# Another order for the first four k-tiles of a two-layer decoder trunk

## The chip, the cores and the metric

The kernel runs on one core of one Trainium2 chip. The metric is the device time of one execution in microseconds; lower is better. A core has TensorE (matrix products into PSUM), VectorE, ScalarE and GpSimd (elementwise work) and SyncE, whose queue issues the DMA transfers here. Each engine runs its instructions in the order in which they stand in its queue and waits at semaphores for the others. In the profile PE is TensorE, PEld its weight loads, DVE VectorE, ACT ScalarE, POOL GpSimd and SPq the DMA issues of SyncE. L508 is line 508 of the kernel.

## What is computed

Two layers on x of 512 tokens by 2048 features, in float32. The opening, which is what the change touches, is the first layer's input projection with an adaptive shift and scale:

```python
c_act = jax.nn.silu(c)
mod = c_act @ w_mod[l] + b_mod[l]
shift, scale, gate = jnp.split(mod, 3, axis=-1)
h = x * (1.0 + scale[:, None]) + shift[:, None]
# layer 0, inside diff_attention:
proj = h @ w_in                              # 2048 x 8192
q, k, v, g = jnp.split(proj, 4, axis=-1)     # 8 heads; then attention, out projection
x = layer_norm(DN_ALPHA * x + gate[:, None] * y, ln_g[l], ln_b[l])
```

Layer 0 goes on with differential attention, an output projection and a layer norm; then come shared keys, values and forget gates and a second layer of attention.

## The kernel before

*Products.* The 2048 input features are 16 k-tiles of 128. To keep float32 accuracy each operand is split into an upper part, rounded to the fast matmul type, and a lower part, the rest; a product is three matmuls, upper-upper, upper-lower and lower-upper (L173, L174, L175, `products`). The upper part of a weight is a ScalarE cast (`whi`, L93), the lower a VectorE subtraction (`wlo`, L94), both in `WeightStream.step`, for two k-tiles at a time. Weights stream from memory through four staging buffers `wst` (loads at L46); `whi` and `wlo` have three buffers each.

*Shift and scale.* c_act @ w_mod is a sum over 16 k-tiles of rows of w_mod, each weighted by one column of c_act. The 16 k-tiles of output columns are cut into nine sets: sets 0 and 1 make one k-tile's shift and scale each, sets 2 to 8 two. A set's rows come in two or four tiles `sms` (L454; five buffers). VectorE multiplies each of the 16 row blocks by its column of c_act and adds (L479, L481, `sacc`; below, a step). TensorE then sums `sacc` over the partitions with a column of ones (L511, "last sums") and VectorE adds the bias (`mcol`, L517). In set 1 eight of the 16 row blocks are not done on VectorE but on TensorE, as matmuls of 128 by 128 with one column of c_act (L508, `on_pe`); such a matmul appears as two loads and two matmuls in the trace.

*h.* A k-tile of x (loaded as `xt`, L430) is turned by four transposes into PSUM (L522, `turn_x`); ScalarE applies shift and scale twice, to the upper part `hh` (L526) and to `htmp` (L527), and VectorE subtracts for the lower part `hl` (L531, `lower_h`).

*The opening's order.* Two head groups (u = 0 and 1) are computed there, each with seven accumulators of 512 columns in seven of the eight PSUM banks: three for q and k (banks `sc`, `sc`, `o`), four for v and gate (`acc`). One k-tile of one group is 7 accumulators by 3 matmuls, 21. Because the banks hold one group at a time, work runs in five phases, (group, first k-tile, end): (0, 0, 4), (1, 0, 8), (0, 4, 12), (1, 8, 16), (0, 12, 16). At a phase's end the accumulators are spilled: copied to SBUF by ScalarE the first time (L559), added by VectorE later (L561). The eighth bank, `tr`, serves transposes and sums.

VectorE's instructions run in the order in which the program writes them. That order is the string START: a digit is so many steps of the shift and scale sums, `c` the sums of the next set on TensorE, `m` its columns, `t` the turn of the next k-tile of x (with its set's sums, if they are still to be done), `l` a lower part of h, `s` the split of the next weights, `g` the products of the next k-tile of the running phase. All other engines are put in order by a planner from the program's order and its own estimates of time.

The mark T4, which the prediction uses, is the start of the first matmul of phase (1, 0, 8), that is, the end of the first four k-tiles of group 0.

## Time and profile before

| | us |
|---|---|
| median of 3 runs (2008.10 to 2009.01) | 2008.82 |
| the profiled execution, its own time | 2007.0 |
| its span, first to last instruction | 2005.2 |
| TensorE busy in it | 1964.4 (98%) |
| VectorE busy in it | 1336.4 (67%) |
| GpSimd busy in it | 2.2 |

How to read what the prediction shows. A row of a timeline is: start, length, engine, line, operation, what is written and read with shapes, how many instructions, and in brackets the idle time before it and what ended it. Lengths of TensorE are modelled and overlap, so costs are read from starts. A row of a table by stretches is: stretch, its length, then busy time and instruction count of PE, PEld, DVE, ACT and POOL, then the granted TensorE clock (1.00 is full), the mean busy share of the DMA engines and GB/s. A row without brackets whose engine field is followed directly by a tile's name ("PE tr L511 x8") is a piece of the chain of work that ended last: start, length, engine, tile, line, count.

### The profile page before, as it was taken

The numbers are of one execution on the slowest core, as the hardware profiler recorded it, in microseconds if no ns is written. First come the engines' busy times: TensorE is split into PE (matmuls) and PEld (weight loads), VectorE is DVE, ScalarE is ACT, GpSimd is POOL, SyncE is SP. The second block draws the span as 40 slices with busy tenths as digits, with TensorE's granted clock in tenths as the row PEclk, the third lists the DMA queues.
The fourth block names the chain that finished last, engine by engine and source line by source line (L and its number), as shares of the span: only waits on it lengthen the run. The fifth ranks groups of instructions, "written<-read, shape, count | busy, mean of one in ns | idle before, by whom it ended". The sixth has DMA issues, their size and how long they took to land.

```text
span 2005.2 us, 25007 instructions
## 1 busy us (share of the span) xinstructions
PE 1964.4 (98%) x9115; PEld 1626.3 (81%) x9115; DVE 1336.4 (67%) x2435; ACT 725.0 (36%) x1234; POOL 2.2 (0%) x10
## 2 busy tenths in 40 slices
PE   5999999999999999999999999999999999999997
PEld 4888878888888888888878888888888888888885
DVE  7887865677777778853576666635455555576778
ACT  2422445333333334431263222224343334353132
POOL 0000000000000000000000000000000000000000
PEclk8999999999999999999999999999999999999999
DMA  9994742375757666453336687634323232333755
GB/s 343 347 315 145 243 151 85 106 230 185 225 178 231 189 223 213 158 166 100 121 137 223 234 276 260 225 95 129 103 90 105 95 102 93 96 120 97 257 190 175
DMA packets 263095, 353.79 MB, mean 176 GB/s; under 512 B 18022, under 2 KB 162556, under 8 KB 262204
## 3 DMA queue, kind: packets, MB, share of 16 engines
q1 hardware_dynamic: 260592, 347.99, 53.2%
q10 hardware_dynamic: 2380, 4.21, 0.6%
q8 instruction: 71, 1.16, 0.2%
q14 instruction: 52, 0.43, 0.1%
...
## 4 chain that ended last, share of the span: by engine, by line
PE 90%; DVE 4%; DMA 3%; SPq 1%; issue 1%; ACT 0%; DVEq 0%; ACTq 0%
PE acc L173 26%; PE acc L174 26%; PE acc L175 26%; DMA ms<-in_w_mod_dram 2%; PE sc L173 2%; PE sc L174 2%; PE sc L175 2%; PE o L175 1%; PE o L174 1%; PE o L173 1%; PE tr L1200 1%; DVE macc L391 1%; DVE wlo L94 1%; DMA sms<-in_w_mod_dram 1%; PE tr L727 0%
## 5 line engine op out<-in xcount | busy, mean ns | idle before, releaser
L94 DVE TENSOR_TENSOR wlo<-wst,whi 128x1024 fp32r<-128x1024 f32 (+2 forms) x339 | 404.7, 1196 | 278.3 <-ACT whi L93 266.8
L93 ACT CAST whi<-wst 128x1024 fp32r<-128x1024 f32 (+2 forms) x339 | 349.6, 1032 | 641.0 <-PE acc L175 323.0
L173 PE MATMUL acc<-whi,hh 128*128 128x512 f32 x1252 | 491.7, 396 | 0.9 <-ACT hh L967 0.8
L174 PE MATMUL acc<-wlo,hh 128*128 128x512 f32 x1252 | 489.1, 391 | 0.0
L175 PE MATMUL acc<-whi,hl 128*128 128x512 f32 x1252 | 488.2, 390 | 0.0
L173 PE MATMUL acc<-hh,whi 128*128 128x512 f32 x1184 | 470.4, 397 | 1.1 <-DVE sg L680 0.6
L175 PE MATMUL acc<-hh,wlo 128*128 128x512 f32 x1184 | 462.3, 390 | 0.0
L174 PE MATMUL acc<-hl,whi 128*128 128x512 f32 x1184 | 462.2, 390 | 0.0
L391 DVE SCALAR_TENSOR_TENSOR macc<-ms,cact,macc 128x512 f32<-128x512 f32 x300 | 225.0, 750 | 78.7 <-DMA ms<-in_w_mod_dram 53.8
L175 PEld LDWEIGHTS acc<-whi,hl 128*128 128x128 f32 x1252 | 235.3, 188 | 50.7 <-DVE hl L968 0.3
L173 PEld LDWEIGHTS acc<-whi,hh 128*128 128x128 f32 x1252 | 235.7, 188 | 48.5 <-ACT hh L967 1.2
L174 PEld LDWEIGHTS acc<-wlo,hh 128*128 128x128 f32 x1252 | 235.6, 188 | 46.4 <-DVE wlo L94 0.4
L175 PEld LDWEIGHTS acc<-hh,wlo 128*128 128x128 f32 x1184 | 222.3, 188 | 48.6
L173 PEld LDWEIGHTS acc<-hh,whi 128*128 128x128 f32 x1184 | 222.6, 188 | 43.8 <-PE acc L175 1.0
L174 PEld LDWEIGHTS acc<-hl,whi 128*128 128x128 f32 x1184 | 222.8, 188 | 39.3
L481 DVE SCALAR_TENSOR_TENSOR sacc<-sms,cact,sacc 128x512 f32<-128x512 f32 (+1 forms) x127 | 89.5, 705 | 5.2 <-DMA sms<-in_w_mod_dram 1.5
L710 ACT ACTIVATE e<-e,mn 128x128 f32<-128x128 f32 (+3 forms) x64 | 36.0, 563 | 126.2 <-DVE mn L706 126.0
L1189 ACT ACTIVATE eb<-eb,mnb 128x128 f32<-128x128 f32 (+1 forms) x64 | 36.1, 563 | 96.8 <-DVE mnb L1186 95.7
L1186 DVE CUSTOM_DVE_ANT_0 eb<-sc,biasb 128x128 f32<-128x128 f32 (+1 forms) x64 | 31.4, 490 | 52.7 <-PE sc L175 52.7
L391 DVE SCALAR_TENSOR_TENSOR macc<-msk,cact,macc 128x512 f32<-128x512 f32 x60 | 44.5, 750 | 14.5 <-DMA msk<-in_w_mod_dram 13.4
L1204 DVE TENSOR_TENSOR pTl<-tr,pTh 128x128 fp32r<-128x128 f32 (+1 forms) x64 | 31.2, 488 | 26.5 <-ACT pTh L1203 26.2
L706 DVE CUSTOM_DVE_ANT_0 e<-sc,bias 128x128 f32<-128x128 f32 (+3 forms) x64 | 31.1, 486 | 21.3 <-PE sc L175 21.2
...
## 6 DMA issues: line engine op xcount, KB each, us to landing
wst<-in_a_w_in_dram SPq DMA_DIRECT2D x240, 256.0 KB
...
wst<-in_b_w_in_dram SPq DMA_DIRECT2D x128, 256.0 KB
...
```

What stands on the lines that cost most here:

```text
L93: self.nc.scalar.copy(hi[:, :, :w], st[:, :, :w])
L94: self.nc.vector.tensor_tensor(lo[:, :, :w], st[:, :, :w], hi[:, :, :w].bitcast(F32), op=ALU.subtract)
L173: PE.matmul(dst, lhs[0], rhs[0], start=start, stop=False)
L174: PE.matmul(dst, lhs[0], rhs[1], start=False, stop=False)
L175: PE.matmul(dst, lhs[1], rhs[0], start=False, stop=stop)
L391: V.scalar_tensor_tensor(acc, w, cact[:, kt : kt + 1], acc, op0=ALU.mult, op1=ALU.add)
L481: V.scalar_tensor_tensor(acc, w, sc, acc, op0=ALU.mult, op1=ALU.add)
L706: V.tensor_tensor_reduce(out=e[:, :w], in0=sc[:, :w], in1=st["bias"][:, (3 - i) * P :], scale=-1.0, scalar=3.0e38, op0=ALU.add, op1=ALU.mi ...
L710: S.activation(e[:, :w], e[:, :w], AF.Exp, bias=mn, scale=-1.0, accum_out=rs)
L1186: V.tensor_tensor_reduce(out=e[:, :w], in0=sc[:, :w], in1=bias[:, :w], scale=-1.0, scalar=3.0e38, op0=ALU.add, op1=ALU.min, accum_out=mn)
L1189: S.activation(e[:, :w], e[:, :w], AF.Exp, bias=mn, scale=-1.0, accum_out=rs)
L1204: V.tensor_tensor(pTl[:, 0 : i + 1, ts], src, pTh[:, 0 : i + 1, ts].bitcast(F32), op=ALU.subtract)
```

## The change

The first four k-tiles of group 0, with sets 0 to 2, no longer come out of START and the planner. They are written out, and in that stretch TensorE and ScalarE, too, run in program order.

- Sets 0, 1 and 2 are summed by both engines as tiles arrive, in four groups of row blocks each: set 0 eight blocks on VectorE and eight on TensorE, set 1 ten and six, set 2 eleven and five. Each group's TensorE sums go to a column of their own, the VectorE part to a fifth; a reduction over the five and the bias give the columns (`group_columns`).
- `fill` puts matmuls of 256 columns with zeros between the groups: 5, 5, 5 and, after the last sums, 6 in set 0; none in set 1; 6, 8 and at the end 6 in set 2. They write columns of the bank that holds the sums, which nothing reads.
- x of k-tile 0 is turned before its columns are known, k-tiles 1 to 3 one or two k-tiles ahead, and kept as copies by ScalarE (`keep_x`).
- The weights of these k-tiles are loaded and split one k-tile at a time, and the 21 matmuls of a k-tile run as all upper-upper, then those with the lower weights, then those with the lower h.
- x of the first four k-tiles comes in three transfers instead of two, and the order of the transfers changes.
- From k-tile 4 on a new START rules. Every second lower part of weights (even numbers from 4 to 26, those of q and k, 128 by 768) is computed on GpSimd. A spill that adds is done at the next `g` or where `A` stands.

```diff
-START = "cmtlssg6c6t1lgcst4g3tsl9sggts8sl6s2gtggts7lgsstlgg2s7gstl2ss9gsgtslgg5stgg6lsstg2gss8sggt2g4l4sgstctslggtslssggssgggg"
+START = (
+    "s3sggs9sggs4t3t2sgslg9s2t2tgs2lg3sggs9tstggs3l6sggs7t2stgs2lg8sAggs4tstggs3l5sggs8tstgslgsAggssgg"
+)
 LAM_INIT = 0.8 - 0.6 * math.exp(-0.0)
...
+    def load_one(self, nc, dst, kt):
+        rows = self.src[kt * P : (kt + 1) * P, :]
+        off = 0
+        for c, n in self.parts:
+            nc.sync.dma_start(dst[:, kt % 2, off : off + n], rows[:, c : c + n])
+            off += n
...
+    def load_halves(self, k):
+        for n in range(2 * (k // 2), 2 * (k // 2) + 2):
+            job, s = self.order[n]
+            if k % 2 == 0:
+                self.stage.append(self.pool.tile([P, 2, 512], F32, name="wst", tag="wst", bufs=self.STAGES))
+            job.load_one(self.nc, self.stage[n], k)
+    def split_half(self, n, k):
+        job, s = self.order[n]
+        if k == 0:
+            hi = self.pool.tile([P, 2, 512], F32R, name="whi", tag="whi", bufs=3)
+            lo = self.pool.tile([P, 2, 512], F32R, name="wlo", tag="wlo", bufs=3)
+            self.subs[(id(job), s)] = tuple([t[:, q, :] for q in range(2)] for t in (hi, lo))
+            self.done += 1
+        hi, lo = (t[k] for t in self.subs[(id(job), s)])
+        w, st = job.width, self.stage[n]
+        return (
+            lambda: self.nc.scalar.copy(hi[:, :w], st[:, k, :w]),
+            lambda: self.nc.vector.tensor_tensor(lo[:, :w], st[:, k, :w], hi[:, :w].bitcast(F32), op=ALU.subtract),
+        )
+    def step(self, extra=None, on_pool=False):
         job, s = self.order[self.done]
         self.load(self.done + 1)
         st = self.stage[self.done]
         w = job.width
+        lower = self.nc.gpsimd if on_pool else self.nc.vector
...
-            self.nc.vector.tensor_tensor(lo[:, :, :w], st[:, :, :w], hi[:, :, :w].bitcast(F32), op=ALU.subtract)
+            lower.tensor_tensor(lo[:, :, :w], st[:, :, :w], hi[:, :, :w].bitcast(F32), op=ALU.subtract)
...
-        def on_pe(i):
-            return 8 if i == 1 else 0
...
-                if k == 0:
-                    if k0 == 0:
-                        load_x(0, 0, P)
-                    elif k0 == 1:
-                        load_x(0, P, T)
-                    elif k0 % 4 == 0:
-                        load_x(k0 // 4, 0, T)
+                if i > 2 and k == 0 and k0 % 4 == 0:
+                    load_x(k0 // 4, 0, T)
...
-        def mod_steps():
+        def mod_step(i, k):
+            k0, nk = sets[i]
+            nr = 8 // nk
+            w, sc = loaded[i, k // nr * nr][:, k % nr, :, :], cact[:, k : k + 1]
+            if i not in accs:
+                accs[i] = sp.tile([P, 2, 2 * P], F32, name="sacc", tag="sacc", bufs=2)[:, :, : nk * P]
+                V.tensor_scalar(accs[i], w, sc, None, op0=ALU.mult)
+            else:
+                V.scalar_tensor_tensor(accs[i], w, sc, accs[i], op0=ALU.mult, op1=ALU.add)
...
-                    for k in range(KT - on_pe(i), KT):
-                        kr = k // nr * nr
-                        PE.matmul(
-                            dst, loaded[i, kr][:, k - kr, v, js], cact[:, k : k + 1], start=k == KT - on_pe(i), stop=False
-                        )
-                    PE.matmul(dst, accs[i][:, v, js], ones[:, 0:1], start=on_pe(i) == 0, stop=True)
+                    PE.matmul(dst, accs[i][:, v, js], ones[:, 0:1], start=True, stop=True)
...
-        def turn_x(kt):
+        def transpose_x(kt):
             px = tr_bank()
             for b in range(TB):
                 PE.transpose(px[:, b * P : (b + 1) * P], xts[kt // 4][:, b, (kt % 4) * P : (kt % 4 + 1) * P], ident)
+            return px
+        def h_steps(kt, src):
             new_h(kt)
             tmp = sp.tile([P, T], F32, name="htmp", tag="htmp", bufs=2)
             sh, sc = mcol[:, 0, kt : kt + 1], mcol[:, 1, kt : kt + 1]
-            S.activation(Hh[kt], px, AF.Identity, scale=sc, bias=sh)
-            S.activation(tmp, px, AF.Identity, scale=sc, bias=sh)
+            return tmp, [
+                lambda dst=dst: S.activation(dst, src, AF.Identity, scale=sc, bias=sh) for dst in (Hh[kt], tmp)
+            ]
+        def turn_x(kt):
+            tmp, steps = h_steps(kt, transpose_x(kt))
+            for step in steps:
+                step()
             return tmp
...
-        at = {"set": 0, "kt": 0, "go": 0}
-        summed, turned = [], []
...
         def go():
             u, kt, start, stop = todo[at["go"]]
+            add_up()
             while at["kt"] <= kt:
                 turn()
             if turned and turned[0][0] <= kt:
                 lower()
             first_products(u, kt, start, stop)
+            at["go"] += 1
             if stop:
-                spill(u)
-            at["go"] += 1
+                full.append((u, at["go"] - 1))
+                if u not in part or at["go"] == len(todo):
+                    add_up()
+        def add_up():
+            if full:
+                spill(*full.pop())
         def split_next():
             if ws.done < 32:
-                ws.step()
+                ws.step(on_pool=ws.done % 2 == 0 and ws.done < 27)
                 ws.load(ws.done + 3)
...
+        def group_sums(i, pm, c, ks):
+            k0, nk = sets[i]
+            nr = 8 // nk
+            for v in range(2):
+                for j in range(nk):
+                    col = 5 * (nk * v + j) + c
+                    for k in ks:
+                        PE.matmul(
+                            pm[:, col : col + 1], loaded[i, k // nr * nr][:, k % nr, v, j * P : (j + 1) * P],
+                            cact[:, k : k + 1], start=k == ks[0], stop=k == ks[-1],
+                        )
+        def last_sums(i, pm):
+            k0, nk = sets[i]
+            for v in range(2):
+                for j in range(nk):
+                    col = 5 * (nk * v + j) + 4
+                    PE.matmul(
+                        pm[:, col : col + 1], accs[i][:, v, j * P : (j + 1) * P], ones[:, 0:1], start=True, stop=True
+                    )
+        def group_columns(i, pm):
+            k0, nk = sets[i]
+            red = sp.tile([P, 4], F32, name="mred", tag="mred", bufs=2)[:, : 2 * nk]
+            V.tensor_reduce(
+                red, pm[:, : 10 * nk].rearrange("p (s c) -> p s c", c=5), axis=mybir.AxisListType.X, op=ALU.add
+            )
+            V.tensor_tensor(
+                mcol[:, :, k0 : k0 + nk], red.rearrange("p (v j) -> p v j", v=2), bcol[:, :, k0 : k0 + nk], op=ALU.add
+            )
+        def sums_at(i, pm, dve, pe, fills=(0, 0, 0, 0), between=None):
+            for c in range(4):
+                for k in dve[c]:
+                    mod_step(i, k)
+                group_sums(i, pm, c, pe[c])
+                if c == 1 and between:
+                    between()
+                fill(fills[c], pm)
+            last_sums(i, pm)
+        warm = kpool.tile([P, T], F32R, name="warm", tag="K")
+        S.activation(warm, mask, AF.Copy, scale=0.0)
+        def fill(n, pm):
+            for _ in range(n):
+                PE.matmul(pm[:, 256:512], warm[:, 0:P], warm[:, 0:256], start=True, stop=True)
+        def ordered_products(kt, between=None):
+            if kt == 0:
+                acc[0] = [acc_bank() for _ in range(4)] + [sc_bank(), sc_bank(), o_bank()]
+            start, stop, q = kt == 0, kt == 3, kt % 2
+            (qhi, qlo), (vhi, vlo) = ((t[q] for t in ws.subs[(id(j), kt // 2)]) for j in first[0])
+            bs = [slice(b * P, (b + 1) * P) for b in range(4)]
+            for part, (wq, hq, wv, hv) in enumerate(
+                ((qhi, Hh[kt], vhi, Hh[kt]), (qlo, Hh[kt], vlo, Hh[kt]), (qhi, Hl[kt], vhi, Hl[kt]))
+            ):
+                if part == 2 and between:
+                    between()
+                for b in range(3):
+                    PE.matmul(acc[0][4 + b], wq[:, bs[b]], hq, start=start and part == 0, stop=stop and part == 2)
+                for b in range(4):
+                    PE.matmul(acc[0][b], hv[:, bs[b]], wv, start=start and part == 0, stop=stop and part == 2)
+        raw_x = {}
+        def keep_x(kt):
+            px = transpose_x(kt)
+            raw_x[kt] = kpool.tile([P, T], F32, name="xT", tag="K")
+            S.copy(raw_x[kt], px)
...
+        load_mods(1)
+        load_x(0, 0, P)
+        load_mods(2)
+        ws.load_halves(0)
+        load_mods(3)
+        load_x(0, P, 2 * P)
+        load_mods(4)
+        ws.load_halves(1)
+        load_x(0, 2 * P, T)
+        load_mods(5)
+        with tc.manual_schedule(engines={ET.PE, ET.Activation}):
+            px = []
+            pm = acc_bank("pm0")
+            sums_at(
+                0, pm, ((0, 1), (4, 5), (8, 9), (12, 13)), ((2, 3), (6, 7), (10, 11), (14, 15)), (5, 5, 5, 0),
+                lambda: px.append(transpose_x(0)),
+            )
+            fill(6, pm)
+            load_mods(7)
+            group_columns(0, pm)
+            (q_hi, q_lo), (v_hi, v_lo) = ws.split_half(0, 0), ws.split_half(1, 0)
+            tmp, (h_hi, h_tmp) = h_steps(0, px[0])
+            q_hi()
+            h_hi()
+            v_hi()
+            h_tmp()
+            q_lo()
+            mod_step(1, 0)
+            mod_step(1, 1)
+            v_lo()
+            lower_h(0, tmp)
+            ordered_products(0, lambda: keep_x(1))
+            pm = tr_bank()
+            sums_at(1, pm, ((2,), (4, 5), (8, 9, 10), (12, 13)), ((3,), (6, 7), (11,), (14, 15)))
+            load_mods(8)
+            ws.load_halves(2)
+            ws.load_halves(3)
+            (q_hi, q_lo), (v_hi, v_lo) = ws.split_half(0, 1), ws.split_half(1, 1)
+            q_hi()
+            v_hi()
+            q_lo()
+            group_columns(1, pm)
+            tmp, (h_hi, h_tmp) = h_steps(1, raw_x[1])
+            h_hi()
+            h_tmp()
+            v_lo()
+            ws.load(6)
+            load_mods(9)
+            mod_step(2, 0)
+            lower_h(1, tmp)
+            ordered_products(1, lambda: keep_x(2))
+            keep_x(3)
+            pm = tr_bank()
+            sums_at(
+                2, pm, ((1, 2), (4, 5, 6), (8, 9, 10), (12, 13)), ((3,), (7,), (11,), (14, 15)), (0, 6, 8, 0)
+            )
+            fill(6, pm)
+            (q_hi, q_lo), (v_hi, v_lo) = ws.split_half(2, 0), ws.split_half(3, 0)
+            q_hi()
+            v_hi()
+            q_lo()
+            group_columns(2, pm)
+            tmp, (h_hi, h_tmp) = h_steps(2, raw_x[2])
+            h_hi()
+            h_tmp()
+            v_lo()
+            lower_h(2, tmp)
+            (q_hi, q_lo), (v_hi, v_lo) = ws.split_half(2, 1), ws.split_half(3, 1)
+            tmp, (h_hi, h_tmp) = h_steps(3, raw_x[3])
+            q_hi()
+            h_hi()
+            v_hi()
+            h_tmp()
+            q_lo()
+            v_lo()
+            lower_h(3, tmp)
+            ordered_products(2)
+            ordered_products(3)
+        for s in range(2):
+            for j in first[0]:
+                ws.subs.pop((id(j), s))
+        spill(0, 3)
+        ws.load(8)
+        steps = mod_steps(3)
+        ahead = [next(steps)]
...
-            elif tok == "c":
-                if at["set"] < len(sets):
-                    sums()
-            elif tok == "m":
-                columns()
...
+            elif tok == "A":
+                add_up()
```

29 lines of the change are left out of this document (9 added, 20 removed).

## The prediction

> **What bounds the kernel now.** I read the page's busy shares first, then busy time by stretches of 10 us, then the start in order of time.
>
> ```profile
> span 2005.2 us, 25007 instructions
> PE 1964.4 (98%) x9115; PEld 1626.3 (81%) x9115; DVE 1336.4 (67%) x2435; ACT 725.0 (36%) x1234; POOL 2.2 (0%) x10
> ...
> 0.00:10.00 10.00, 0.54 (x2) 0.36 (x2) 4.69 (x14) 1.50 (x2) 1.60 (x9) 1.00 0.72 211
> 10.00:20.00 10.00, 3.68 (x12) 2.94 (x13) 5.24 (x12) 3.33 (x4) 0.00 (x0) 1.00 1.10 353
> 20.00:30.00 10.00, 9.27 (x55) 8.08 (x53) 9.56 (x16) 0.00 (x0) 0.00 (x0) 0.96 1.10 379
> 30.00:40.00 10.00, 7.79 (x21) 5.94 (x22) 7.11 (x11) 3.22 (x4) 0.00 (x0) 0.53 1.09 385
> 40.00:50.00 10.00, 8.19 (x43) 6.49 (x42) 8.88 (x14) 3.73 (x5) 0.00 (x0) 1.00 1.08 385
> 50.00:60.00 10.00, 10.00 (x50) 8.43 (x49) 9.35 (x15) 5.29 (x9) 0.00 (x0) 1.00 1.09 383
> ```
>
> TensorE (the first busy column) is the bound, at 98%; it is idle only at the two ends. The DMA share is full from 10 us on. From 50 us on TensorE is full, so what the opening can win is what it wins before that. I measure it by one mark, T4: the moment when the 84 wide products of the first four k-tiles are done and the first product of head group 1 starts.
>
> ```profile
> 14.53 0.99 PE L511 MATMUL tr<-ones,sacc 128*128 128x1 f32 x4 [11.21 <-DVE sacc L481]
> 18.42 1.22 PE L173 MATMUL sc<-hh,whi 128*128 128x512 f32 x2 [0.87 <-ACT hh L526]
> 22.89 0.62 PE L173 MATMUL acc<-whi,hh 128*128 128x512 f32 x2
> 24.97 1.98 PEld L508 LDWEIGHTS tr<-cact,sms 128*128 128x128 f32 x16
> 27.09 1.87 PEld L508 LDWEIGHTS tr<-cact,sms 128*128 128x128 f32 x16
> 30.63 1.11 PE L522 MATMUL tr<-ident,xt 128*128 128x128 f32 x4 [1.37 <-DVE mcol L517]
> 33.33 1.22 PE L173 MATMUL sc<-hh,whi 128*128 128x512 f32 x2 [1.58 <-ACT hh L526]
> 43.83 0.73 PE L173 MATMUL sc<-hh,whi 128*128 128x512 f32 x2 [0.87 <-ACT hh L526]
> 49.69 0.39 PE L174 MATMUL acc<-wlo,hh 128*128 128x512 f32 x1
> 54.67 0.39 PE L175 MATMUL acc<-whi,hl 128*128 128x512 f32 x1
> 54.90 0.39 PE L173 MATMUL sc<-hh,whi 128*128 128x512 f32 x1
> ...
> 29.00:30.00 1.00, 0.27 (x3) 0.18 (x2) 0.96 (x2) 0.00 (x0) 0.00 (x0) 0.62 1.09 386
> 32.00:33.00 1.00, 0.00 (x0) 0.00 (x0) 0.00 (x0) 1.00 (x2) 0.00 (x0) 0.50 1.09 373
> 39.00:40.00 1.00, 1.00 (x5) 0.77 (x4) 0.96 (x2) 0.00 (x0) 0.00 (x0) 0.76 1.04 406
> ```
>
> T4 is 54.90 us. The k-tiles 0, 1 and 2 start at 18.42, 33.33 and 43.83. At the full clock wide products start 0.227 us apart (22 of them from 49.69 to 54.67), so a k-tile (21) costs 4.77; at half clock they start 0.43 apart.
>
> The clock is the other cost. The first pair took 1.22 us, the pair at 22.89 0.62: half clock until about 22.4. It falls at 29.24 (0.62 in that microsecond) and is back at 39.48 (0.76). The changes are 6.8 and 10.2 us apart, two and three steps of 3.41. On that grid the step 25.83 to 29.24 held only one-column sums and ended in a fall; the steps 19.0 to 22.4 and 36.1 to 39.5 had products throughout and ended in a rise; the step from 32.65 had products only from 33.33 (80%) and did not rise.
>
> **The change, step by step.** The prices of its pieces:
>
> ```profile
> 5.70 0.35 DVE L479 TENSOR_SCALAR sacc<-sms,cact 128x256 f32<-128x256 f32 x1 [1.51 <-DMA sms<-in_w_mod_dram]
> 7.83 2.05 DVE L481 SCALAR_TENSOR_TENSOR sacc<-sms,cact,sacc 128x256 f32<-128x256 f32 x4 [0.22 <-DMA sms<-in_w_mod_dram]
> 10.25 4.13 DVE L481 SCALAR_TENSOR_TENSOR sacc<-sms,cact,sacc 128x256 f32<-128x256 f32 x8 [0.36 <-DMA sms<-in_w_mod_dram]
> 15.96 0.35 DVE L479 TENSOR_SCALAR sacc<-sms,cact 128x256 f32<-128x256 f32 x1 [1.58 <-DMA sms<-in_w_mod_dram]
> 16.23 0.15 DVE L517 TENSOR_TENSOR mcol<-tr,bcol 128x2 f32<-128x2 f32 x1
> 17.59 0.78 ACT L526 ACTIVATE hh<-tr,mcol 128x512 fp32r<-128x512 f32 x1 [2.03 <-PE tr L522]
> 52.61 1.07 ACT L559 COPY part<-sc 128x512 f32<-128x512 f32 x2 [4.97 <-PE sc L175]
> 58.91 0.79 PE tr L511 x8
> 62.14 0.44 PE tr L522 x4
> 7.95 2.23 SPq L46 DMA_DIRECT2D wst<-in_a_w_in_dram  x4
> ```
>
> *Arrivals.* Set 1's first half tile is 3.8 MB down the queue and was used at 15.96, when the stretches had moved 4.2: data are usable some 0.45 MB behind the bytes moved. In the new order set 0's halves still come at 5.7, 7.8, 10.25 and about 12.0, all of set 1 by 20.0 (5.18 MB), set 2 by 33.6 (10.4 MB), the weights of k-tiles 2 and 3 by 36.0.
>
> *Set 0.* VectorE loses 8 of its 16 steps (0.51 each) and is done at 13.1 instead of 14.4. TensorE gets 16 sums. A sum is two loads: nine take 27.09 - 24.97 = 2.12, so 0.236 at the full clock, and 0.46 at half (four loads and matmuls, two sums, in 0.99 to the last end). A fill has half the columns of a product: 0.12, or 0.21 at half. At half clock four sums and five fills take 1.85 + 1.07 = 2.9 us against 2.2 between arrivals, so from 5.7 on TensorE has no idle time: sums 7.55, fill 8.6, sums 10.45. This decides the case: does such a mixture bring the clock up? Low end of its price: yes, in the first whole step, between 9.1 and 12.5. High end: no, only products do. I take the low end, at 10.8, because both rises in the trace followed a step without any idle time, and the one step that failed had 0.68 us of it. The fall after pure sums speaks against it; that step had no wide matmul at all, here fills and the turn of x are about half. From 10.8: x turned 10.95, fill 11.55, sums 12.5, fill 13.1, sums 14.05, two last sums 14.5. Six more fills stand in the sums' own PSUM bank ahead of its reader, so the columns wait for them too: 15.2. Reduce and add (0.15 each, hand-overs) 0.45, hh 0.78 and 0.05: first product at 16.5, not 18.42. The four transposes (1.11) that stood between columns and hh are now ahead.
>
> [...]
>
> *k-tile 0*: 4.77 and one turn, 0.44: 21.7. *Set 1*: 12 + 2 sums, 3.3 (before 18 sums, 4.2): 25.0; columns and hh 1.28: 26.3. These 4.6 us have no fill; a clock step without a wide matmul lies in them for 1.2/3.41, 35% of the phases, so I take no fall, and the other end is 4.5 us at half clock, 2.3. *k-tile 1* and two turns: 31.95. The second turn's bank is also that of the next sums; its copy by ScalarE (1.07 for two, and hand-overs) is waited for, 0.65: 32.6. *Set 2*: 24 sums at 0.79/4, 4.8, 14 fills, 1.7, six more, 0.7: 39.8, behind the data (33.6); columns and hh: 41.1. *k-tiles 2 and 3*: 42 products, 9.53. T4 = 50.6: **4.3 us earlier**. The other copies of turned x, the extra splits and the reduces are on ScalarE and VectorE, which were 3 to 4 and 7 to 9 tenths busy there; if that cover goes, each copy costs its 0.53 once.
>
> *SyncE.* Weights of the four k-tiles come as 16 transfers for 8, x as one more: nine issues of 0.56, 5 us. They hide because 3.28 MB had been issued at 10.2 us and 2.1 moved. Without that, each four halves (0.46 MB) issue in 2.2 us for 1.2 of transfer: set 2 would be 2 us late, within the 3 that its last group of sums now lies behind its data. Set 2's second tile waits for set 0's buffer, with weights queued behind; it is free before 12.5 and asked for after 15.
>
> *After T4.* VectorE runs in written order: four steps of set 3, then the lower part of group 1's first v weights. Its upper part needs the third staging buffer, which k-tile 3 holds until T4 - 0.8, and ScalarE has seven copies of sums to do.
>
> ```profile
> 54.04 2.09 ACT L559 COPY part<-acc 128x512 f32<-128x512 f32 x4
> 55.95 1.11 ACT L93 CAST whi<-wst 128x1024 fp32r<-128x1024 f32 x1
> 51.54 6.26 DVE L481 SCALAR_TENSOR_TENSOR sacc<-sms,cact,sacc 128x512 f32<-128x512 f32 x8
> 46.70 1.22 DVE L94 TENSOR_TENSOR wlo<-wst,whi 128x1024 fp32r<-128x1024 f32 x1
> 50.07 0.95 DVE L94 TENSOR_TENSOR wlo<-wst,whi 128x768 fp32r<-128x768 f32 x1
> 1.35 0.52 POOL L183 MEMSET mask<- 128x512 f32 x1
> 1.94 0.29 POOL L184 TENSOR_SCALAR_AFFINE_SELECT mask<-mask 128x128 f32<-128x128 f32 x1
> ...
> 240.00:260.00 20.00, 18.64 (x95) 15.40 (x95) 18.68 (x50) 10.39 (x24) 0.00 (x0) 1.00 0.58 185
> ```
>
> If ScalarE does the copies first, as above, VectorE goes on at T4 + 3.5. It then has 28 steps of 0.77 to the end of set 4, four lower parts of 1.13, two of h (0.69) and a wait for columns: 29, so T4 + 32.5, and k-tile 6 is ready at T4 + 34.9 after sums, turn and hh. TensorE has six k-tiles and the sums and turns of sets 3 and 4, T4 + 31.5: a stall of 3.4. With the cast ahead of the copies it is under 1. In the kernel before, the last eight of set 3's steps start at 51.54, so 12 were done by T4 and nothing shows the stall. No order is written for ScalarE there, so I take none and make 3.4 a rival. GpSimd takes 12 lower parts of 128x768 off VectorE (0.95 each); TensorE gains nothing, as it did not wait. A lower part on GpSimd is bounded by 0.78 (the memset's 0.52 for 512) and 1.74 (the select's 0.29 for 128); its first result is wanted only at T4. Phase changes and everything behind them I cost at nothing: the same products, sums and adds. Where VectorE is nearly full after the opening (18.68 of 20 us from 240), TensorE idles 1.36; if the lighter VectorE takes that away, it is 1.4 less, an end for the range.
>
> Sum: -4.3 us. The profiled execution took 2007.0 us (span 2005.2 and 1.8 around it) and becomes 2002.7; the median of the runs shown is 1.8 higher, 2008.82, so the forecast is **2004.5 us**.
>
> **Rivals.** *Won and given back (0.13).* The stall before k-tile 6, 3.4: 2007.9. For it: ScalarE's copies did go before the cast at 55.95. Against it: VectorE is rid of every second lower part.
>
> *Cold until the products (0.18).* Only wide products count as activity, as the step of 80% suggests. Set 0's sums, fills and turn take until 18.35, six fills until 19.6, the first product comes at 20.95, the clock rises near 26 (a whole step later), k-tile 0 ends at 28.6, k-tile 1 at 38.8, set 2's columns give hh at 48.0, T4 = 57.5: 2.6 lost, 2011.4. The fall at 29.24 speaks for it. In it the change does not do what it says: the sums on TensorE cost more than they spare.
>
> *The clock falls again (0.15), the slower side.* Cold as before, and the narrow sums of set 1 and of set 2 (fills are a quarter of it) each end in a fall. After set 1 about 4.5 us of products run at half, +2.3; set 2's last 12 sums double, +2.4, and its products pay +1.9: 2018.0. It decides from the first fall on: with one it is 2013.7.
>
> *GpSimd holds VectorE up (0.09).* Three lower parts run there before k-tile 6 is due; at 1.74 each, with VectorE standing meanwhile, the stall of 3.4 grows by 5.2: 2013.1. For it speaks that VectorE is nearly full, against it that the lower parts are short. [...]
>
> **How the numbers follow.** The forecast's case has 0.45; its own range is 2001.5 (rise 1 us earlier, no wait for the copy, the 1.4 won behind) to 2006.8 (one fall after set 1). A measurement here tells about 0.2%, 4.0 us, from no change: 2004.8 and 2012.8. Faster: 0.40 from the forecast's case. Within: its other 0.05, the 0.13 given back, 0.11 of the cold case, 0.03 of GpSimd's: 0.32. Slower: 0.15 from the second falls, 0.07 of the cold case (with part of the stall), 0.06 of GpSimd's: 0.28. The range is 2000.5 to 2015.5: 1 us below the first for an even earlier rise, and up to the two cases near 2013 with part of the stall; it leaves out most of the case with two falls.
>
> **What would show it.** Right: pairs of products at 0.7 us from the first k-tile on; k-tiles 0, 1 and 2 starting near 16.5, 26 and 41; T4 near 50.6; TensorE full from there past 100 us. Wrong: products 0.43 apart at k-tile 0; a second stretch at half clock after 26 or 39; a gap of TensorE near 82, before k-tile 6 of group 1; VectorE's steps longer than 0.75 beside GpSimd; TensorE waiting on lower parts from GpSimd or on set 2's tiles.

## The result and the profile after

The changed kernel took 2046.14 us (median; 2044.08 to 2047.04), the kernel before beside it 2008.91: a ratio of 1.0182, 95% interval 1.0169 to 1.0194. It is 37 us slower; the forecast was 2004.5 and the range 2000.5 to 2015.5. The profiled execution has a span of 2043.9 against 2005.2.

First the stretches of the opening, changed kernel (columns as in the prediction: us, busy time of PE, PEld, DVE, ACT and POOL, granted clock, DMA share, GB/s):

```profile
10.00:20.00 10.00, 8.67 (x39) 8.31 (x39) 3.60 (x10) 1.91 (x4) 0.00 (x0) 1.00 1.05 318
20.00:30.00 10.00, 10.00 (x52) 8.52 (x50) 5.64 (x11) 2.09 (x4) 0.00 (x0) 1.00 1.07 365
30.00:40.00 10.00, 7.96 (x35) 6.31 (x34) 8.73 (x14) 3.03 (x6) 0.00 (x0) 0.83 0.90 294
40.00:50.00 10.00, 10.00 (x55) 10.00 (x55) 1.23 (x3) 0.59 (x2) 0.00 (x0) 0.57 0.70 249
50.00:60.00 10.00, 8.62 (x30) 7.25 (x30) 5.40 (x9) 4.58 (x7) 1.83 (x1) 0.57 0.20 50
60.00:70.00 10.00, 9.98 (x45) 7.96 (x44) 2.95 (x4) 5.18 (x9) 0.19 (x1) 1.00 1.08 378
```

The clock column reads 1.00 until the first change that the trace records, here a rise at 24.4; before it the first products stand 0.43 apart, half clock. It falls at 31.2, rises at 34.7, falls at 41.5 and rises at 58.6: the changes are 6.8, 3.4, 6.8 and 17.1 apart, two, one, two and five steps of a grid of 3.41. From 40 to 60 the clock is 0.57 and the DMA share goes down to 0.20; VectorE works 1.2 of the 10 us from 40 to 50. The kernel before had a clock of 1.00, VectorE at nearly 9 of 10 and the DMA full there. The marks, out of the timelines of TensorE and VectorE:

```profile
16.48 1.63 PE L691 MATMUL pm<-warm 128*128 128x256 f32 x6
19.43 1.22 PE L706 MATMUL sc<-hh,whi 128*128 128x512 f32 x2 [1.33 <-ACT hh L548]
31.67 1.22 PE L706 MATMUL sc<-hh,whi 128*128 128x512 f32 x2 [1.36 <-ACT hh L548]
46.40 3.41 PE L651 MATMUL tr<-cact,sms 128*128 128x1 f32 x16
51.37 1.63 PE L691 MATMUL tr<-warm 128*128 128x256 f32 x6
54.38 1.22 PE L706 MATMUL sc<-hh,whi 128*128 128x512 f32 x2 [1.38 <-ACT hh L548]
65.96 0.39 PE L207 MATMUL sc<-hh,whi 128*128 128x512 f32 x1
...
18.14 0.17 DVE L668 TENSOR_REDUCE mred<-pm 128x2 f32<-128x10 f32 x1 [4.77 <-PE pm L691]
53.04 0.18 DVE L668 TENSOR_REDUCE mred<-tr 128x4 f32<-128x20 f32 x1 [11.78 <-PE tr L691]
```

k-tile 0 starts 1.0 later than before, k-tile 1 1.7 earlier, k-tile 2 10.6 later; T4 is 65.96 instead of 54.90. All three first pairs take 1.22, half clock. What releases VectorE's reduce is the last of the fills (L691), which stand behind the sums; at set 2 it waits 11.8 us for sums and fills together, the last 1.6 of it for six fills.

That is 11 of 38.7. The rest lies before a second mark, the first q0l on VectorE, with which the attention part begins. Its rows, and one stretch from T4 to it, before and then changed:

```profile
204.74 0.68 DVE L662 SCALAR_TENSOR_TENSOR q0l<-part,q0h 128x512 fp32r<-128x512 f32 x1
54.90:204.74 149.84, 149.36 (x704) 123.58 (x702) 119.86 (x170) 52.59 (x74) 0.56 (x1) 1.00 0.78 263
```

```profile
240.15 0.68 DVE L856 SCALAR_TENSOR_TENSOR q0l<-part,q0h 128x512 fp32r<-128x512 f32 x1
65.96:240.15 174.19, 159.29 (x703) 128.75 (x702) 132.89 (x166) 53.25 (x76) 24.75 (x12) 0.95 0.71 237
```

The same TensorE work took 149.84 and 174.19: 24.35 more, of which 14.4 is idle time (174.19 - 159.29, less the 0.48 idle before) and 9.9 longer busy time for the same work. The clock is at half from 89.3 to 92.7, 102.9 to 113.2 and 171.2 to 174.6; TensorE is busy for 14.8 us of these, so half clock is 7.4 of the 9.9. The other 2.5 stays open; the lengths of TensorE are modelled, and a part like it, 1.2 to 1.4, is there in two kernels below whose clock is full throughout (h2 and j1). Behind the mark the two are alike, 1800.5 and 1803.8. So 11.1 in the opening, 24.4 in the stretch, 3.3 behind. VectorE was busy 13.0 us longer in the stretch (132.89 against 119.86), and GpSimd, nearly idle before (0.56), 24.75.

### The profile page after: what moved, and what is told of

It is laid out like the page before. It is cut to its first block, busy times and chain, and to the rows that moved or that the text cites. A ratio compares the mean times of both kernels' runs of the same rounds, so it can differ in the third digit from the quotient of the medians.

```text
span 2043.9 us, 25242 instructions
## 1 busy us (share of the span) xinstructions
PE 1999.1 (98%) x9220; PEld 1656.0 (81%) x9220; DVE 1338.5 (65%) x2419; ACT 727.2 (36%) x1242; POOL 28.4 (1%) x22
## 4 chain that ended last, share of the span: by engine, by line
PE 88%; DVE 7%; DMA 3%; issue 1%; ACT 1%; SPq 0%; DVEq 0%; ACTq 0%
PE acc L207 25%; PE acc L209 25%; PE acc L208 25%; DMA ms<-in_w_mod_dram 2%; DVE sacc L502 2%; DVE wlo L128 1%; PE sc L207 1%; PE sc L208 1%; PE sc L209 1%; PE o L208 1%; PE o L207 1%; PE o L209 1%; PE tr L1394 1%; DMA sms<-in_w_mod_dram 1%; PE acc L708 1%
## 5 line engine op out<-in xcount | busy, mean ns | idle before, releaser
L128 DVE TENSOR_TENSOR wlo<-wst,whi 128x1024 fp32r<-128x1024 f32 (+2 forms) x323 | 390.9, 1211 | 284.5 <-ACT whi L127 282.9
L208 PE MATMUL acc<-wlo,hh 128*128 128x512 f32 x1236 | 482.5, 391 | 1.8 <-DVE wlo L128 1.7
L209 PE MATMUL acc<-whi,hl 128*128 128x512 f32 x1236 | 481.3, 390 | 0.0
L502 DVE SCALAR_TENSOR_TENSOR sacc<-sms,cact,sacc 128x512 f32<-128x512 f32 (+1 forms) x116 | 99.2, 855 | 6.9 <-DMA sms<-in_w_mod_dram 3.7
L904 ACT ACTIVATE e<-e,mn 128x128 f32<-128x128 f32 (+3 forms) x64 | 36.1, 564 | 126.0 <-DVE mn L900 125.8
L1383 ACT ACTIVATE eb<-eb,mnb 128x128 f32<-128x128 f32 (+1 forms) x64 | 36.1, 564 | 96.7 <-DVE mnb L1380 95.6
L1398 DVE TENSOR_TENSOR pTl<-tr,pTh 128x128 fp32r<-128x128 f32 (+1 forms) x64 | 31.2, 487 | 26.8 <-ACT pTh L1397 26.5
```

Of the source, the lines that this page charges most:

```text
L128: lower.tensor_tensor(lo[:, :, :w], st[:, :, :w], hi[:, :, :w].bitcast(F32), op=ALU.subtract)
L208: PE.matmul(dst, lhs[0], rhs[1], start=False, stop=False)
L209: PE.matmul(dst, lhs[1], rhs[0], start=False, stop=stop)
L502: V.scalar_tensor_tensor(accs[i], w, sc, accs[i], op0=ALU.mult, op1=ALU.add)
L904: S.activation(e[:, :w], e[:, :w], AF.Exp, bias=mn, scale=-1.0, accum_out=rs)
L1383: S.activation(e[:, :w], e[:, :w], AF.Exp, bias=mn, scale=-1.0, accum_out=rs)
```

## The experiments

"Stretch" is T4 to q0l. Times are medians; T4 and stretch come from one profiled execution each, and T4 of kernels with the same opening scatters by 3.4, one step of the clock's grid. It follows the place of the grid, which differed between these executions: with the opening of e4, the first rise is at 17.73 (h1), 18.21 (h2), 20.58 (f4), 21.00 (g3), 21.39 (e4) and 22.09 (f2), and T4 comes in the same order, 55.91, 56.40, 58.07, 58.42, 58.68 and 59.27. So a difference in T4 of less than about 3 between two kernels shows nothing.

| kernel | us | ratio to before, interval | T4 | stretch |
|---|---|---|---|---|
| before | 2008 to 2010 | 1 | 54.90 | 149.8 |
| changed | 2046.14 | 1.0182 [1.0169, 1.0194] | 65.96 | 174.2 |
| e1 tiles first | 2045.89 | 1.0186 [1.0171, 1.0202] | 66.14 | 174.9 |
| e2 no GpSimd | 2037.32 | 1.0141 [1.0126, 1.0157] | 66.14 | 167.8 |
| e3 parameters early | 2052.71 | 1.0220 [1.0203, 1.0237] | 67.08 | 179.7 |
| e4 no fill | 2039.55 | 1.0152 [1.0137, 1.0167] | 58.68 | 175.9 |
| f1 = e4, sums on VectorE | 2033.56 | 1.0123 [1.0106, 1.0140] | 56.84 | 175.9 |
| f2 = e4 + e2 | 2029.40 | 1.0105 [1.0090, 1.0121] | 59.27 | 166.8 |
| f3 before + GpSimd | 2019.05 | 1.0055 [1.0040, 1.0070] | 55.08 | 157.9 |
| f4 = f2 + e1 | 2029.30 | 1.0106 [1.0091, 1.0121] | 58.07 | 165.8 |
| g2 = e1, nine steps moved | 2039.26 | 1.0149 [1.0134, 1.0164] | 65.46 | 169.1 |
| g3 = f4, nine steps moved | 2030.41 | 1.0109 [1.0092, 1.0126] | 58.42 | 168.3 |
| g4 = g3, sums on VectorE | 2029.20 | 1.0099 [1.0083, 1.0115] | 56.10 | 170.0 |
| g5 = g4, clock held | 2028.25 | 1.0099 [1.0084, 1.0114] | 55.81 | 168.9 |
| h1 = f4, nine steps ahead | 2029.90 | 1.0106 [1.0091, 1.0121] | 55.91 | 166.7 |
| h2 = f4, old order | 2016.05 | 1.0044 [1.0027, 1.0061] | 56.40 | 153.5 |
| h3 = g5, old order, gap filled | 2011.69 | 1.0021 [1.0011, 1.0031] | 53.84 | 156.5 |
| i2 changed, old order | 2041.67 | 1.0168 [1.0150, 1.0187] | 64.33 | 170.6 |
| i3 = h3, split sooner | 2015.36 | 1.0033 [1.0020, 1.0046] | 52.82 | 158.9 |
| j1 = i2 + e2 | 2022.45 | 1.0065 [1.0047, 1.0083] | 64.84 | 153.2 |

### One part undone: queues, GpSimd, fills

SyncE's queue had two holes in the changed kernel: one from 40 to 56, where a weight load waits for a staging buffer with set 3's tiles behind it, and one of 17.2 us at 105, behind the parameters' loads. e1 loads the tiles first, e3 asks for the parameters sooner:

```diff
# e1
         spill(0, 3)
-        ws.load(8)
         steps = mod_steps(3)
         ahead = [next(steps)]
+        ws.load(8)
# e3: load_parameters() is called ahead of the weight stream, no longer behind the opening
# e2
-                ws.step(on_pool=ws.done % 2 == 0 and ws.done < 27)
+                ws.step()
# e4
-            for _ in range(n):
+            for _ in range(0):
                 PE.matmul(pm[:, 256:512], warm[:, 0:P], warm[:, 0:256], start=True, stop=True)
```

> One edit to the changed kernel: the first tiles of sets 3 and 4 are asked for ahead of the weights that wait for a staging buffer. Queue theory (SyncE stood behind those weights from 39.9 to 56.3 us and left DMA empty from 47 to 57, and this is what starves the rest): the hole is gone, T4 stays near 66 us, the stalls of TensorE between 80 and 110 shrink, and the time falls by 8 to 18 us from 2046. Clock theory (the loss is half clock before T4 and what follows from it): T4 near 66 and the time within 3 us of 2046. GpSimd theory: as the clock theory.

> One edit to the changed kernel: the seven small parameter loads on ScalarE's queue are issued at the start instead of behind the opening. Queue theory, second place (SyncE's next shift and scale tile stood from 105.5 to 123 behind one of these loads, DMA empty from 110 to 124): that hole is gone, the late sums and phase changes after 140 us come earlier, and the time falls by 4 to 12 us. If the hole is only there because nothing was needed: within 2 us.

e1: 2045.89, no change; the first hole went and the DMA was nearly idle from 60 to 70 instead (82 GB/s). e3: 2052.71, worse; the second hole went (DMA share 0.58 from 110 to 120 instead of 0.00), but the first product came 2.5 later, T4 1.1 later, and the stretch was 5.5 longer, for a reason that I did not follow up. The queue theory fell: taking away either hole gained nothing.

> One edit to the changed kernel: all lower parts of weights on VectorE. GpSimd theory (each lower part of 2.0 to 2.3 us on GpSimd holds VectorE up by about 1.5 us, more than the 0.95 that it spares): VectorE's steps take 0.77 us apart everywhere, and the time falls by 4 to 10 us. If GpSimd's work is free to VectorE: 12 x 0.95 = 11 us more work on VectorE, and the time is the same or up to 8 us longer. Queue and clock theories: within 3 us, T4 near 66.

> One edit to the changed kernel: no fill matmuls at all. If the fills do nothing for the clock, as the trace suggests (no rise before 24.5 us, a fall at 41.6): k-tile 0 starts 4 to 5 us earlier (15 fills and 6 ahead of the columns, 0.21 each), k-tile 2 another 4, T4 falls to 57 to 60, and the time by 6 to 12 us. If the fills are what raised the clock at 24.5: k-tile 0 earlier, but the rise later and T4 at 62 or more.

e2 gained 8.8; in the profiled executions 6.4 of 6.9 lie in the stretch, and T4 is the same. e4 gained 6.6, all in the opening: T4 58.68, the first product at 15.55 instead of 19.43. This is more than the scatter: T4 is 64.3 to 67.1 in the seven kernels with these fills and 55.9 to 59.3 in the six that lack nothing but them. The clock rose and fell as often without the fills; what they did was to stand in TensorE's queue ahead of sums and of the columns' reader.

### Parts put together, and GpSimd alone

f1 gives all steps of sets 0 to 2 to VectorE (empty lists for TensorE, the columns read the one sum that is left) in e4; f2 is e2 and e4 in one; f4 is f2 with e1. f3 is the kernel before with one edit:

```diff
# f3, on the kernel before (step() gets the argument on_pool)
-                ws.step()
+                ws.step(on_pool=ws.done % 2 == 0 and 4 <= ws.done < 27)
```

> The changed kernel without fills, and with every step of sets 0 to 2 on VectorE instead of half of them on TensorE; order, x turned ahead, halves and GpSimd stay. It differs from e4_no_fill (2039.55) by the place of the sums alone. Theory 'the sums on TensorE cost': they run as narrow products at half clock (6.86 us for 40 of them in set 2 there), so without them k-tile 1 starts at about 22 to 25 instead of 28.16, k-tile 2 at 38 to 42 instead of 46.35, T4 at 49 to 53 instead of 58.68, and the time is 2030 to 2034. Rival 'VectorE is what is short behind T4': VectorE gets some 19 steps more before T4 and none fewer after it, the gain in T4 is waited away before k-tile 6 and the change of phase, and the time stays at 2037 to 2042.

> The changed kernel without fills and with every lower part on VectorE: e2 and e4 in one. Theory 'two separate losses': the gains add, 8.8 and 6.6 off 2046.1, so 2030.7, 2029 to 2033. Rival 'both feed the same wait': the second gain finds the first one's stall gone, and less than 11 of the 15.4 is seen, 2035 or more.

> The kernel before, with the 12 lower parts of the query and key weights on GpSimd and nothing else changed. Theory 'GpSimd costs VectorE more than it saves': each costs the steps beside it about 1.5 us and saves 0.95, 12 of them 6.6 us, of which the slack in the kernel before hides part: TensorE waited 0.5 us there from 55 to 205. 2011 to 2018. Rival 'only a VectorE that is already behind feels it': no more than the uncertainty, 2008 to 2012.

> f2 with the weights' load put behind the first tiles of set 3, as in e1: e1, e2 and e4 in one. Theory 'the hole in the queue costs once the other losses are gone': 3 to 5 below f2, so 2026 to 2028. Rival 'the hole is covered by other work': within 1.5 of f2, 2029 to 2032.

f2: the gains add (2029.4; 2030.7 was expected). f4 equals f2: the place of that load is worth nothing here either. f3: GpSimd alone makes the kernel before 11 us slower, more than the 3 to 10 I had expected. f1: 6 less than e4 by the medians, 2.5 by the profiled spans, 2 of it T4, not the 6 to 9 expected there: VectorE became the engine that was waited for before T4 (TensorE waited 9.5 us for it). What the place of the sums is worth by itself is not shown: 2 us in T4 are within the scatter.

### Nine steps, the clock, and the order

In f4 VectorE stood idle for 8.3 us around T4 behind a weight split. Four kernels were to put nine steps into that hole:

```diff
# g2 (on e1), g3 (on f4); g4, g5 with f1's sums besides
-    "s3sggs9sggs4t3t2s...
+    "s12sggssggs4t3t2s...
# g5 besides: fills of set 2 (0, 6, 8, 0) and six -> (55, 0, 0, 0); no others
```

The edit was wrong. The string is read one character at a time, so 12 is one step and two: three steps ahead of the split as before, and the nine behind both splits, later than before. The expectations speak of an edit that only h1, below, made.

> e1 (the changed kernel with the tiles of set 3 loaded ahead of the weights) with nine steps of set 3 put ahead of the second weight split on VectorE instead of behind it. In e1 and f4 VectorE stands still for about 8.5 us from 53 on, its tiles already there, behind that split's lower part, whose upper part stands on ScalarE behind the seven copies of the sums, which stand behind the products of k-tile 3. Theory 'this hole is what makes VectorE late': the nine steps, 7 to 8 us, go into the hole, the wait before k-tile 6 (6.1 in e1) and half of the half clock behind it go, and the time is 2036 to 2041 against 2045.89 for e1. Rival 'VectorE is short of time throughout': the steps come sooner and the wait moves to the next change of phase, 2043 to 2048.

> The same nine steps moved in f4 (tiles first, no GpSimd, no fills; 2029.3). Theory 'the hole makes VectorE late': TensorE's standstill from 90 to 98 (5.1 us idle and about 5 us at half clock) goes, 2019 to 2024. Rival 'short of time throughout': 2027 to 2031.

> g3 with all steps of sets 0 to 2 on VectorE. Theory 'the sums on TensorE cost in themselves': T4 some 2 earlier as in f1 against e4, and 4 to 6 off g3. Rival 'without GpSimd VectorE is the one that is short before T4': T4 within 1 of g3's and the time within 2.5 of g3's, or longer.

> g4 with 55 fills of 256 columns straight behind the products of k-tile 1, in the stretch of 8.7 us in which f1's TensorE had nothing to do and its clock fell from 1.00 to 0.50 (until 49.6). Theory 'a TensorE that is kept busy without a gap keeps its clock': the fills take 0.11 to 0.14 each at full clock, 6 to 7.7 in all, the clock stays 1.00 up to k-tile 2's products, whose 7 us at half become 4.75, and T4 and the time are 2 to 4 less than g4's. Rival 'fills do not count': the clock falls at about 36 all the same, the fills take 0.27 each from there, and T4 is 1 to 8 later than g4's.

With the nine steps later, g2 was 6.6 faster than e1, and g3 and f4 are equal within their intervals. So these two runs say nothing for the theory, though g2's time lies in its range; that is luck. Why the later place helps with GpSimd in is open. g4 and g3 are equal within their intervals, T4 2.3 apart. g5 is about the clock. Stretches of g3, in which narrow sums fill the wait of set 2:

```profile
36.12 6.95 PE L651 MATMUL tr<-cact,sms 128*128 128x1 f32 x40 [0.67 <-ACT xT L715]
36.00:38.00 2.00, 1.89 (x17) 1.89 (x17) 1.53 (x3) 0.69 (x3) 0.00 (x0) 1.00 0.58 179
38.00:39.00 1.00, 1.00 (x7) 1.00 (x6) 0.72 (x2) 0.51 (x1) 0.00 (x0) 0.53 0.95 281
39.00:42.00 3.00, 3.00 (x16) 3.00 (x15) 0.00 (x0) 0.00 (x0) 0.00 (x0) 0.50 0.82 229
```

and of g5, in which 55 wide fills do:

```profile
35.78 6.86 PE L686 MATMUL tr<-warm 128*128 128x256 f32 x55 [0.67 <-ACT xT L710]
38.00:39.00 1.00, 1.00 (x11) 1.00 (x10) 0.96 (x2) 0.00 (x0) 0.00 (x0) 1.00 0.49 160
39.00:42.00 3.00, 3.00 (x28) 3.00 (x27) 2.06 (x4) 0.84 (x1) 0.00 (x0) 1.00 0.83 214
42.00:44.00 2.00, 1.42 (x14) 1.34 (x12) 0.54 (x2) 0.28 (x1) 0.00 (x0) 1.00 0.85 227
44.00:45.00 1.00, 0.41 (x1) 0.41 (x2) 0.26 (x1) 1.00 (x2) 0.00 (x0) 0.78 1.07 353
45.00:46.00 1.00, 1.00 (x3) 0.74 (x3) 0.73 (x2) 1.00 (x3) 0.00 (x0) 0.50 1.05 363
```

TensorE is busy in both. In g3 the clock falls at 38.1, 2 us into the one-column sums; in g5 it stays at 1.00 through the 6.9 us of wide fills. g5 lost it all the same, at 44.6, after 2.1 us without wide work: its last eight sums, 0.95, and 1.17 idle up to k-tile 2's products. T4 was not the 2 to 4 earlier that I had expected.

h1 makes the edit that was meant, h2 gives f4 the kernel before's own order from T4 on, and h3 gives that order to g5 and fills the gap:

```diff
# h1, on f4
-    "s3sggs9sggs4t3t2s...
+    "s39sggssggs4t3t2s...
# h2, on f4: three steps, a split, nine steps, then the kernel before's string from its fifth g on,
# each phase's copies or sums at its end (A); the token c calls sums() as before
-    "s3sggs9sggs4t3t2sgslg9s2t2tgs2lg3s...
+    "3s9gts8sl6s2gtggts7lgsstlgg2s7gAstl2ss9gsg...
# h3, on g5: h2's string, 44 fills for 55, and
             group_columns(2, pm)
+            fill(9, pm)
```

> f4 (changed kernel, tiles first, no GpSimd, no fills; 2029.3) with nine steps of set 3 really put ahead of the second weight split, into the 8.4 us that VectorE stands idle from 53 on. Theory 'the standstill behind the split makes VectorE late': the idle 5.1 us before k-tile 6 and the half clock behind it go, 2020 to 2025. Rival 'short of time throughout': the wait moves to a later stop and the time is 2027 to 2031.

> f4 with the order of the kernel before from T4 on: 12 steps of set 3 and one split, then that kernel's own string from its fifth group of products, the copies and sums of a phase at its end as there. Theory 'the new order behind the opening costs the rest': T4 stays at 58 to 60, TensorE loses no more than 5 us from T4 to the first q0l (the kernel before: 149.84 for that stretch), and the time is 2010 to 2016. Rival 'something else holds it (queues, VectorE's time)': the stretch stays above 160 and the time at 2022 to 2031.

> g5 (all sums on VectorE, fills straight behind k-tile 1's products, no GpSimd, tiles first) with h2's order, 44 fills instead of 55, and nine fills more between the columns of set 2 and k-tile 2's products. Theory 'the clock fell at 44.8 in g5 for 3.4 us because of the 2.1 us between the last sums and the products alone': with the gap filled the clock stays 1.00 through k-tile 2, T4 is 52.5 to 54.5, and the time some 4 below h2's, 2005 to 2012. Rival 'fills in the gap do not hold it': T4 55 or later and the time within 2 of h2's.

h1: 2029.9 against 2029.3. The steps did run at T4, and VectorE then stood 7.3 us behind a later split and TensorE 4.0 before k-tile 6 as in f4. h2: 2016.05, 13.3 less with the same instructions in another order. How long VectorE waited, and for what, from 55 to 210 us (us in total, times, longest), and the stretch, in f4:

```profile
DVE mcol L535 <- PE tr L529: 14.7, 6, 3.6
DVE wlo L128 <- DMA wst<-in_a_w_in_dram: 8.3, 1, 8.3
DVE wlo L128 <- ACT whi L127: 6.6, 3, 4.2
58.07:223.90 165.83, 155.86 (x703) 126.76 (x702) 125.71 (x177) 54.05 (x76) 0.56 (x1) 0.97 0.73 241
```

and in h2:

```profile
DVE hl L558 <- ACT htmp L548: 7.7, 3, 3.5
DVE wlo L128 <- ACT whi L127: 6.6, 5, 3.7
DVE mcol L535 <- PE tr L529: 6.0, 6, 1.9
56.40:209.90 153.50, 150.75 (x704) 123.17 (x703) 121.85 (x173) 53.70 (x76) 0.56 (x1) 1.00 0.79 263
```

In the new order VectorE waits 14.7 for the columns of later sets, that is for sums that stand on TensorE behind products, and 14.9 behind weight splits (8.3 and 6.6); in f4's 8.3 us, up to 61.4, VectorE ran nothing of what stands behind that split, and its nine steps started at 63.4. In the old order it is 6.0 and 6.6. TensorE's idle time falls from 10.0 to 2.8, and the 10.2 us at half clock in f4 (95.7 to 102.5 and 143.5 to 146.9, 4.7 lost) are gone: from T4 on h2's clock is full up to q0l. Which of the moved tokens does it was not separated, and h1 shows that the longest single wait, the 8.3 us, taken away alone gains nothing.

h3: the gap's nine fills held the clock into k-tile 2's products,

```profile
43.11 1.34 PE L686 MATMUL tr<-warm 128*128 128x256 f32 x9 [0.25 <-DVE mcol L668]
44.00:45.00 1.00, 1.00 (x8) 0.87 (x8) 0.29 (x1) 1.00 (x3) 0.00 (x0) 1.00 0.93 290
45.00:46.00 1.00, 1.00 (x6) 0.83 (x5) 0.87 (x2) 1.00 (x3) 0.00 (x0) 1.00 1.05 345
```

where g5 had 0.78 and 0.50; T4 is 53.84, 1.1 earlier than before in this one execution (i3, with the same opening, has 52.82), and the time 2011.69, 4.4 below h2 with two things changed. It is the best of all kernels run, and still slower than before.

### GpSimd in the old order

i2 is the changed kernel with h2's string and nothing else, j1 is i2 with e2's edit, i3 is h3 with "3s4s5" for "3s9", the second split sooner.

> The changed kernel with one part undone: behind the opening, the order of the kernel before (as in h2), with fills, GpSimd's lower parts and the place of the loads left as changed. Theory 'the order costs by itself': the same 13 as between f4 and h2 come off 2046.1, 2031 to 2036. Rival 'with GpSimd in it VectorE is late in any order': 2038 to 2046.

> h3 (2011.69) with the second weight split after four of the nine steps instead of behind them. Theory 'this wait is a loss of its own': TensorE's 2.7 us at 59 to 62 go, 2008 to 2010. Rival 'VectorE's steps are what is late, and the wait moves on to the columns of set 3': within 1 of h3, 2010.5 to 2012.5.

> i2 with every lower part on VectorE. Theory 'GpSimd is what keeps VectorE late in the old order': h2's 2016 and 6.6 for the fills, 2020 to 2025, that is 17 to 21 below i2. Rival 'the loads' place or the fills matter more than they did in the new order': 2026 to 2034.

i2: 2041.67, only 4.5 less: with GpSimd in, VectorE is late in the old order too. j1: 2022.45, 19.2 less than i2. VectorE's and GpSimd's groups from 64 us to q0l (busy time, mean ns of one, idle time before and what ended it), i2:

```profile
L502 DVE SCALAR_TENSOR_TENSOR sacc<-sms,cact,sacc 128x512 f32<-128x512 f32 x87 | 80.2, 922 | 5.6 <-DMA sms<-in_w_mod_dram 3.1
L128 DVE TENSOR_TENSOR wlo<-wst,whi 128x1024 fp32r<-128x1024 f32 (+2 forms) x19 | 21.1, 1108 | 14.6 <-ACT whi L127 12.7 <-DMA ms<-in_w_mod_dram 1.3 <-DMA sms<-in_w_mod_dram 0.5
L128 POOL TENSOR_TENSOR wlo<-wst,whi 128x768 fp32r<-128x768 f32 x11 | 24.7, 2246 | 103.1 <-ACT whi L127 68.3 <-DMA sms<-in_w_mod_dram 18.1 <-DVE hl L558 16.7
64.33:234.90 170.57, 160.60 (x704) 130.10 (x703) 131.88 (x166) 53.42 (x76) 25.22 (x12) 0.94 0.73 244
```

and j1:

```profile
L502 DVE SCALAR_TENSOR_TENSOR sacc<-sms,cact,sacc 128x512 f32<-128x512 f32 x87 | 65.3, 751 | 6.2 <-DMA sms<-in_w_mod_dram 3.8
L128 DVE TENSOR_TENSOR wlo<-wst,whi 128x1024 fp32r<-128x1024 f32 (+2 forms) x30 | 31.2, 1051 | 4.4 <-ACT whi L127 4.3
64.84:218.06 153.22, 150.60 (x703) 123.14 (x702) 125.99 (x177) 53.64 (x76) 0.56 (x1) 1.00 0.81 271
```

The eleven lower parts save VectorE 10.1 us and cost its 87 steps 14.9, because a step takes 922 ns instead of 751 on average. So VectorE has 4.8 us more to do, and TensorE pays 17.4 in the stretch: 7.4 of idle time (i2 10.0, j1 2.6) and 10.0 of longer busy time. i2's granted clock of 0.94 over the stretch is some 20 us at half clock, j1's 1.00 none; half of that, about 10, is an estimate of what it costs at the most, as much as the 10.0.

i3: 2015.36, outside both expectations and 3.7 above h3, though single times of the two overlap. TensorE's wait of 2.7 us for the split, at 62, was gone; it waited 1.5 for a later split, 2.6 for set 3's and 4's sums and 1.8 at 208 for a phase's adds instead.

By these runs the 37 us are, in one order of undoing: 4.5 the order (i2), 19.2 GpSimd (j1), 6.4 the fills with the load's place (h2), and 7 to 8 what is left of the new opening. The shares depend on the order of undoing. From the changed kernel, undoing GpSimd alone gains 8.8 (e2), the order alone 4.5 (i2), both 23.7 (j1): each makes VectorE late, so undoing only one of them gains less. Without GpSimd and the fills the order is worth 13.3 (f4 and h2). Of h2's rest, 1.5 is T4, 3.7 the stretch, and the remainder lies behind q0l, where the profiles of all kernels scatter from 1799.7 to 1805.9; it stays open.

## Why the prediction was wrong

*T4.* The mark was right, its value was not: 50.6 forecast, 65.96 measured.

- *Set 0*: the step that failed first is the low end of the mixture's price. Fills, sums and turns did not raise the clock: in the grid's steps from 7.35 to 17.59 TensorE had no idle time and fills for 1.1 to 1.7 of each 3.41 us. The first product came at 19.43 at half clock, not at 16.5, and the clock rose at 24.4, behind the first step full of products. That is the rival *Cold until the products* (20.95, near 26). The six fills ahead of the columns, 0.7 in the prediction, took 1.63.
- *Set 1*: "I take no fall" was wrong. The clock fell at 31.2, after a step of 2.5 us of sums and 0.9 of idle time, and k-tile 1 started at 31.67 instead of 26.3.
- *Set 2*: the term that was mis-sized most. 24 sums and 20 fills were 7.2 at full clock; they took from 39.71 to 53.0, 13.3, mainly because the clock fell at 41.5 and stayed down until 58.6. A smaller slip: these sums were priced at 0.20 us each where sets 0 and 1 had 0.236, 0.9 us in all. k-tile 2 started at 54.38, not 41.1. The rival *The clock falls again* had T4 = 64.1 with two falls, within 2 us.
- The row that should have decided is quoted in the prediction: the step of one-column sums that ended in a fall. I set it aside because it held no wide matmul at all; but the step that ended in the fall at 41.5 held no fill either, since set 2's first six stand behind its second group of sums, at 41.56. Those that came then, 5.3 of set 2's 13.3 us, did not raise the clock again. In g2 a step with 0.9 us of fills and 2.5 of sums (40.9 to 44.3) ended in a fall too; 6.9 us of fills alone held the clock in g5.
- *The range*: its lower end counts a rise 1 us earlier than the 10.8 of the forecast, and one earlier still. No run shows a rise so early: it came at 24.4 in the changed kernel and between 17.73 (h1) and 22.09 (f2) in the six kernels with e4's opening.

*Arrivals* held up to set 2; then the queue stood still behind a load waiting for a buffer, which the step *SyncE* did not price. e1 and f4, which took the hole away, were no faster.

*After T4.* "Phase changes and everything behind them I cost at nothing" is, together with GpSimd below, the step that failed with the greatest price: 24.4 us, of which 21.0 go when order and GpSimd are both undone (j1's stretch, 153.2). I compared which instructions there are and not where each stands: the products, sums and adds are the same, but VectorE waits for columns and splits in another place, and the place alone is worth 13.3 (h2). That "12 steps were done by T4 and nothing shows the stall" held the hint: the kernel before comes to T4 with its order already ahead. That a later start is not made good behind it because VectorE is nearly full is a reading that no run tested by itself. The stall before k-tile 6 that I put at 0 to 3.4 is there, 3.1 (6.1 in e1, 4.0 in f4), and *Won and given back* was right about its place and far too small, since a larger one follows at a later phase, where TensorE waits for VectorE's adds:

```profile
104.06 1.84 PE L529 MATMUL tr<-ones,sacc 128*128 128x1 f32 x8 [3.09 <-DVE sacc L502]
171.20 0.77 PE L207 MATMUL sc<-hh,whi 128*128 128x512 f32 x1 [4.77 <-DVE part L588]
```

The clock falls at 102.9 and at 171.2, beside both.

*GpSimd* at no cost is the other. It was bounded at 0.78 to 1.74 for one lower part; it takes 2.0 to 2.5. The rival *GpSimd holds VectorE up* let VectorE stand while each of three of them runs, 5.2; that it stands was an assumption of mine that no trace of before shows. That VectorE is held was right and the count was not: in the changed kernel each of the 12 holds one VectorE instruction. Eleven times it is a step, which takes 2.21 to 2.33 instead of 0.75 and ends 0.55 us behind the lower part; once it is a lower part of VectorE's own. So each costs VectorE some 1.46 us and spares it 0.95, and the runs give 8.8 to 19.2 for all of them. Three steps that take 2.32 without GpSimd take 3.79 beside one lower part of 2.02, and the lower parts take 2.25 on average in i2's group above, more than the upper bound of 1.74.

```profile
58.17 2.02 POOL L128 TENSOR_TENSOR wlo<-wst,whi 128x768 fp32r<-128x768 f32 x1 [55.94 <-DVE hl L558]
58.53 3.79 DVE L502 SCALAR_TENSOR_TENSOR sacc<-sms,cact,sacc 128x512 f32<-128x512 f32 x3
158.32 2.07 POOL L128 TENSOR_TENSOR wlo<-wst,whi 128x768 fp32r<-128x768 f32 x1 [9.15 <-ACT whi L127]
158.73 2.21 DVE L502 SCALAR_TENSOR_TENSOR sacc<-sms,cact,sacc 128x512 f32<-128x512 f32 x1
```

```profile
71.67 2.32 DVE L502 SCALAR_TENSOR_TENSOR sacc<-sms,cact,sacc 128x512 f32<-128x512 f32 x3
```

(The first four rows are of the changed kernel, the last of h1, which has no lower parts on GpSimd.)
